# Decay-row loads of a state-space stage, issued from GpSimd's queue instead of SyncE's

## The chip, the cores and the metric

The kernel is one program on one core of a Trainium2 chip. Five engines run their own instruction streams in order and meet at semaphores: TensorE (PE, with its weight loads shown as PEld), VectorE (DVE), ScalarE (ACT), GpSimd (POOL) and SyncE (SP). The metric is the device time of one execution in microseconds (us); before the change the median of three runs was 1223.0 us (1222.05 to 1225.13). All data is float32, and products are made with the input split into a high and a low part (`split`), so that one float32 product is three matmuls.

## The reference

One decoder layer with two token mixers on 1024 tokens of width 1024. The part that the change touches is the state-space branch: 16 heads of 64, state size 64, chunks of 128 tokens.

```python
a_cs = jnp.cumsum(ac, axis=-1)                       # per head and chunk
seg = a_cs[..., :, None] - a_cs[..., None, :]
lmat = jnp.exp(jnp.where(tril, seg, -jnp.inf))       # decay between two tokens of a chunk
cb = jnp.einsum("bclgn,bcsgn->bgcls", cc, bc)
y_diag = jnp.einsum("bgrcls,bcsgrp->bclgrp", cb[:, :, None] * lmat, xc)
decay_states = jnp.exp(a_cs[..., -1:] - a_cs)
states = jnp.einsum("bclgn,bgrcl,bclgrp->bcgrpn", bc, decay_states, xc)
...                                                  # states carried from chunk to chunk
y_off = jnp.einsum("bclgn,bcgrpn,bgrcl->bclgrp", cc, prev_states, jnp.exp(a_cs))
y = y_diag + y_off + d_skip * xs
```

Around it stand the input norm and the input projection to 8472 columns ahead of it, and behind it attention with forget gates, the projections of both branches, gates, the output projection and a last norm.

## The kernel before

The program runs in stages: norm and first projections (to about 100 us), the other projections as Strassen-like pair products (to about 480 us), the state-space stage with the last projections mixed in (about 480 to 722 us), attention (to about 930 us) and the output products. A scheduler places all instructions of the build into one order per engine by a timeline of its own, with priorities; an engine then runs its list strictly in order. The state-space stage has priority 300 over the rest (`tc.high_priority(offset=SPRI)`), and projection slabs of v, q and k (`fill`, called from `FILL`) give TensorE work between its steps.

The stage's work is 4 groups of heads (`qd`), each of 2 halves (`hf`), each of 4 chunks (`c`): 32 chunks in all, done by `ssd_half`. One chunk goes like this.

- `ab` (128x512, 3 buffers) is filled from DRAM (`a_scr`) with the four decay rows of the chunk, copied to all 128 partitions (L688). ScalarE makes four relus (L690) and one exp (L692) of it, VectorE multiplies it with `cb` (L693), and `split` turns it into `m4`: a cast on ScalarE (L98) and a subtraction on VectorE (L99, `m<-ab,m`). That subtraction is the last reader of the `ab` buffer, and so releases it for the chunk three later.
- TensorE transposes the chunk of x (`xs`) into `xps` (L698). VectorE makes `xd` (L707) and `xe` (L710) of it, and both are split.
- L718 makes the chunk's addition to the state, L724 updates the state `st32` on VectorE, and `sn` is its split (cast on ScalarE, subtraction on VectorE). The next chunk's L746 and L747 need `sn`.
- L735 makes the part inside the chunk (12 small matmuls), L746 and L747 the part from the state carried over. VectorE multiplies the latter with `eb` (L748) and adds the former (L751). `eb` (2 buffers) holds decay rows too, loaded by two DMAs for each chunk but the first of a group (L740), 56 in all.

After a half, VectorE adds the skip (L779), multiplies by the gate (L780) and sums the squares (L785, `sacc`). After the last half TensorE adds these up in two groups of columns (L791, shown as 8 instructions each), VectorE scales (L794), GpSimd takes a power (L796), TensorE transposes (L798), and the result goes out and comes back as `rb` for the attention stage.

All DMAs of the program are issued from SP. In the stage these are the loads of `ab`, `eb`, `xs`, `zt` (the gate) and `wr` (weights of the projection slabs), and the stores of results. SP waits, at each issue, until the buffer is free and the DMA that used the same completion semaphore before has landed; what stands behind waits too. GpSimd has nothing to do between 30 us and L796 at 722.7 us.

Of the kernel before, what the change touches and what calls it, by code (L numbers as in the profile page):

```python
# [31 lines left out]
P = 128  # L32
# [33 lines left out]
def build(ctx, tc, t):  # L66
    nc = tc.nc
    V, A, G, PE, SP = nc.vector, nc.scalar, nc.gpsimd, nc.tensor, nc.sync
# [88 lines left out]
    a_scr = dram.tile([P, P], F32, name="a_scr")  # L157
# [479 lines left out]
    with tc.tile_pool(name="sd", bufs=1, side="right") as sd, \  # L637
            tc.tile_pool(name="sdp", bufs=1, space=PSUM) as sdp:

        def sp():  # L640
            return sdp.tile([P, 512], F32, tag="sp", bufs=4, name="sp")
# [36 lines left out]
        def ssd_half(qd, hf, xs, ys, st32, sn):  # L678
# [3 lines left out]
            for c in range(4 * hf, 4 * hf + 4):  # L682
                tk = slice(c * P, (c + 1) * P)
                th = slice((c % 4) * P, (c % 4 + 1) * P)
                r0 = c * 16 + 4 * qd
                m4 = sd.tile([P, 2, 4, P], F32R, tag="m4", bufs=3, name="m4")
                ab = sd.tile([P, 4, P], F32, tag="ab", bufs=3, name="ab")
                SP.dma_start(out=ab, in_=a_scr[r0:r0 + 4].rearrange("(o h) l -> o h l", o=1).broadcast_to([P, 4, P]))  # L688
                for i in range(4):
                    A.activation(out=ab[:, i, :], in_=ab[:, i, :], func=AF.Relu, scale=-1.0,  # L690
                                 bias=acs[:, c, 4 * qd + i:4 * qd + i + 1])
# [39 lines left out]
                for i in range(4):  # L731
                    o = yd[0:64, (i % 2) * 256 + (i // 2) * P:(i % 2) * 256 + (i // 2) * P + P]
# [4 lines left out]
                if c > 0:  # L737
                    eb = sd.tile([P, 2, P], F32, tag="eb", bufs=2, name="eb")
                    for z in range(2):
                        SP.dma_start(out=eb[z * 64:(z + 1) * 64],  # L740
                                     in_=e_scr[r0:r0 + 4].rearrange("(r two) l -> two r l", two=2)[z:z + 1]
                                     .broadcast_to([64, 2, P]))
                    yo = sp()
                    for i in range(2):
                        ps_ = slice(i * P, (i + 1) * P)
                        PE.matmul(yo[:, ps_], lhsT=so[:, ps_], rhs=ch[g][:, tk], start=True, stop=False)  # L746
                        PE.matmul(yo[:, ps_], lhsT=so[:, ps_], rhs=cl[g][:, tk], start=False, stop=True)  # L747
                    V.tensor_tensor(out=ys[:, :, th], in0=yo[:, 0:256].rearrange("p (r l) -> p r l", r=2), in1=eb,  # L748
                                    op=ALU.mult)
                    for z in range(2):  # L750
                        V.tensor_tensor(out=ys[half[z], :, th], in0=yd[z], in1=ys[half[z], :, th], op=ALU.add)  # L751
                else:
                    for z in range(2):
                        A.copy(out=ys[half[z], :, th], in_=yd[z])
# [9 lines left out]
        for qd in range(4):  # L764
            st32, sn = sd.tile([P, 256], F32, tag="st32", bufs=1, name="st32"), None
            for hf in range(2):
                hs = slice(hf * 512, (hf + 1) * 512)
                xs = [sd.tile([P, 512], F32, tag="xs", bufs=5, name="xs") for _ in range(2)]
                for i in range(2):
                    SP.dma_start(out=xs[i], in_=x_scr[2 * qd + i][:, hs])  # L770
                ys = sd.tile([P, 2, 512], F32, tag="ys", bufs=2, name="ys")
                with tc.high_priority(offset=SPRI):
                    sn = ssd_half(qd, hf, xs, ys, st32, sn)
                for i in range(2):
                    j = 2 * qd + i
                    zt = sd.tile([P, 512], F32, tag="zt", bufs=2, name="zt")
                    SP.dma_start(out=zt, in_=z_scr[j][:, hs])
                    y = ys[:, i]
                    V.scalar_tensor_tensor(out=y, in0=xs[i], scalar=dskip[:, j:j + 1], in1=y, op0=ALU.mult, op1=ALU.add)  # L779
                    V.tensor_tensor(out=y, in0=y, in1=zt, op=ALU.mult)  # L780
                    if j == 0:
                        A.activation(out=sacc[:, hs], in_=y, func=AF.Square)
                    else:
                        A.activation(out=zt, in_=y, func=AF.Square)
                        V.tensor_tensor(out=sacc[:, hs], in0=sacc[:, hs], in1=zt, op=ALU.add)  # L785
                    SP.dma_start(out=u_scr[j][:, hs], in_=y)
            for f in FILL[qd]:
                fill[f]()
# [461 lines left out]
```

## Time and profile before

| | |
|---|---|
| median of 3 runs (lowest, highest) | 1223.0 us (1222.05, 1225.13) |
| the profiled execution's own time | 1224.68 us |
| its span (first to last instruction) | 1223.0 us |
| mean granted TensorE clock | 0.987 |
| busy in the span: PE / DVE / ACT / POOL | 95% / 78% / 52% / 7% |
| busy in 600 to 700 us, inside the stage: PE / DVE / ACT / POOL | 94.8% / 93.3% / 67.0% / 0% |

A row of a timeline has the start in us, the duration in us, the engine, the line, the operation, what it writes and reads, how many instructions were merged, and in brackets how long the engine was idle before it and what ended that wait. Matmuls overlap, so that the distance from one start to the next tells TensorE's pace, and the duration does not. Waits are put down to what came last.

### The profile page before, as it was taken

Reading aid. Unit: us, or ns where it says so; the run is one execution under the profiler, and the core shown is the slowest. Engines: PE = TensorE matmul, PEld = TensorE weight load, DVE = VectorE, ACT = ScalarE, POOL = GpSimd, SP = SyncE. Lnnn points to the kernel's source line nnn. Section 1 sums busy time; section 2 is a strip of 40 time slices with the busy share of each in tenths; the row PEclk is TensorE's granted clock in tenths of the full one; section 3 lists DMA queues with packets and bytes.
Section 4 is the critical chain, followed back from the end, with each engine's and each line's share of the span. In section 5 each row is a group of like instructions: output and inputs, shape, how many; then the busy total and the mean of one; then the engine's idle time right before and its main releaser. Section 6 shows DMA issues by size and latency. Waiting matters only on the chain.

```text
span 1223.0 us, 18391 instructions
## 1 busy us (share of the span) xinstructions
PE 1162.5 (95%) x6206; PEld 978.0 (80%) x6206; DVE 952.6 (78%) x1942; ACT 634.6 (52%) x1260; POOL 87.8 (7%) x152
## 2 busy tenths in 40 slices
PE   3999999999999999999998989999989998999997
PEld 2788888788877878998887878888868886788876
DVE  5857699788887774599999976664677967979967
ACT  7554443444453334876676633443556644454465
POOL 1000000000000000000000012222322220000001
PEclk9999999999999999999999989999999999999999
DMA  9764643655485665656555658431255627955334
GB/s 371 262 247 162 220 141 102 208 198 181 151 288 175 229 235 198 195 155 212 186 167 158 220 202 297 138 112 53 91 183 184 190 70 250 326 181 181 104 96 147
DMA packets 109018, 228.26 MB, mean 187 GB/s; under 512 B 12362, under 2 KB 20220, under 8 KB 107900
## 3 DMA queue, kind: packets, MB, share of 16 engines
q1 hardware_dynamic: 108924, 227.09, 55.5%
q8 instruction: 49, 0.80, 0.3%
q14 instruction: 45, 0.37, 0.1%
HBM read 159.14 MB, written 67.90 MB: 186 GB/s over the span
## 4 chain that ended last, share of the span: by engine, by line
PE 71%; DVE 12%; DMA 9%; issue 4%; ACT 3%; SPq 0%; POOL 0%; POOLq 0%; DVEq 0%; ACTq 0%
PE pp L497 5%; PE pp L499 5%; PE pp L500 5%; PE pv L1061 4%; PE mm L497 4%; PE mm L499 4%; PE mm L500 4%; PE mm L112 3%; PE mm L113 3%; PE mm L111 3%; PE lg L1030 3%; PE tp L1051 2%; PE mm L915 2%; PE mm L913 2%; DMA ab<-a_scr 2%
## 5 line engine op out<-in xcount | busy, mean ns | idle before, releaser
L98 ACT CAST wh<-wr 128x512 fp32r<-128x512 f32 (+1 forms) x214 | 131.0, 619 | 172.4 <-DMA wr<-w_c 33.2
L99 DVE TENSOR_TENSOR wl<-wr,wh 128x512 fp32r<-128x512 f32 (+1 forms) x214 | 145.6, 686 | 43.3 <-ACT wh L98 42.8
L112 PE MATMUL mm<-hl,wh 128*128 128x512 f32 x288 | 116.6, 405 | 0.4 <-DVE hl L306 0.4
L111 PE MATMUL mm<-hh,wh 128*128 128x512 f32 x288 | 116.0, 408 | 0.0
L113 PE MATMUL mm<-hh,wl 128*128 128x512 f32 x288 | 115.3, 401 | 0.0
L136 PE MATMUL mm<-wh,hh 128*128 128x256 f32 (+1 forms) x256 | 73.0, 287 | 2.2 <-DVE tmp L348 2.2
L137 PE MATMUL mm<-wl,hh 128*128 128x256 f32 (+1 forms) x256 | 73.7, 289 | 0.0
L138 PE MATMUL mm<-wh,hl 128*128 128x256 f32 (+1 forms) x256 | 73.0, 286 | 0.0
L1036 ACT ACTIVATE pr<-pr,sm 128x1024 f32<-128x1024 f32 (+3 forms) x64 | 49.9, 780 | 43.8 <-DVE sm L1035 36.6
L1054 ACT CAST pth<-tp 128x512 fp32r<-128x512 f32 (+1 forms) x80 | 42.4, 543 | 51.0 <-PE tp L1051 42.7
L1031 DVE CUSTOM_DVE_ANT_0 pr<-lg,fb 128x512 f32<-128x512 f32 (+1 forms) x96 | 51.3, 550 | 18.2 <-PE lg L1030 12.4
L112 PEld LDWEIGHTS mm<-hl,wh 128*128 128x128 f32 x288 | 55.1, 191 | 11.0 <-DVE hl L306 1.0
L113 PEld LDWEIGHTS mm<-hh,wl 128*128 128x128 f32 x288 | 55.0, 191 | 10.4
L111 PEld LDWEIGHTS mm<-hh,wh 128*128 128x128 f32 x288 | 54.7, 192 | 10.2 <-ACT hh L305 0.3
L690 ACT ACTIVATE ab<-ab,acs 128x128 f32<-128x128 f32 x128 | 41.2, 391 | 40.6 <-DMA ab<-a_scr 35.7
L1055 DVE TENSOR_TENSOR ptl<-tp,pth 128x512 fp32r<-128x512 f32 (+1 forms) x80 | 49.9, 630 | 11.1 <-ACT pth L1054 10.7
L1039 POOL TENSOR_SCALAR pr<-pr,sm 128x1024 f32<-128x1024 f32 (+3 forms) x64 | 51.9, 812 | 86.9 <-DVE sm L1038 67.1
L98 ACT CAST sh<-sr 128x512 fp32r<-128x512 f32 x57 | 33.9, 618 | 42.1 <-DVE sr L479 30.6
L796 POOL TENSOR_TENSOR fl<-fl,mhalf 128x8 f32<-128x8 f32 x1 | 1.6, 1647 | 696.5 <-DVE fl L794 696.5
L136 PEld LDWEIGHTS mm<-wh,hh 128*128 128x128 f32 x256 | 48.1, 188 | 2.6 <-DVE tmp L348 2.4
L1061 PE MATMUL pv<-pth,vh 128*128 128x256 f32 (+1 forms) x160 | 45.8, 286 | 4.2 <-DVE zg L1064 3.6
L138 PEld LDWEIGHTS mm<-wh,hl 128*128 128x128 f32 x256 | 48.3, 189 | 0.0
(406 smaller groups left out, 3496.2 us busy)
## 6 DMA issues: line engine op xcount, KB each, us to landing
wr<-w_c SPq DMA_DIRECT2D x116, 256.0 KB, 3.8
wa<-w_ada SPq DMA_DIRECT2D x8, 1024.0 KB, 11.4
g_scr<-gt SPq DMA_DIRECT2D x16, 512.0 KB, 4.0
ab<-a_scr SPq DMA_DIRECT2D x32, 256.0 KB, 4.2
gt<-g_scr SPq DMA_DIRECT2D x32, 256.0 KB, 3.7
wr<-w_ps SPq DMA_DIRECT2D x28, 256.0 KB, 2.8
wr<-w_pa SPq DMA_DIRECT2D x28, 256.0 KB, 2.7
wr<-so SPq DMA_DIRECT2D x28, 256.0 KB, 2.7
```

Of the source, the lines that this page charges most:

```text
L98: A.copy(out=hi[:, :n], in_=raw[:, :n])
L99: eng.tensor_tensor(out=lo[:, :n], in0=raw[:, :n], in1=f32(hi[:, :n]), op=ALU.subtract)
L111: PE.matmul(ps, lhsT=hi[:, cs], rhs=xh[k][:, hs], start=(k == 0), stop=False)
L112: PE.matmul(ps, lhsT=hi[:, cs], rhs=xl[k][:, hs], start=False, stop=False)
L113: PE.matmul(ps, lhsT=lo[:, cs], rhs=xh[k][:, hs], start=False, stop=(k == 7))
L136: PE.matmul(o, lhsT=xh[k][:, ts], rhs=hi[:, cs], start=(k == 0), stop=False)
L137: PE.matmul(o, lhsT=xh[k][:, ts], rhs=lo[:, cs], start=False, stop=False)
L138: PE.matmul(o, lhsT=xl[k][:, ts], rhs=hi[:, cs], start=False, stop=(k == 7))
L497: PE.matmul(ps, lhsT=f[0][:, w], rhs=xh[:, hs], start=(first and k == 0), stop=False, skip_group_check=True)
L499: PE.matmul(ps, lhsT=f[0][:, w], rhs=xl[:, hs], start=False, stop=False, skip_group_check=True)
L500: PE.matmul(ps, lhsT=f[1][:, w], rhs=xh[:, hs], start=False, stop=(k == 3), skip_group_check=True)
L1061: PE.matmul(pv[:, o0:256], lhsT=x[kb // 4][:, kb % 4, vs], rhs=y[:, d:d + m], start=(kb == 0 and i == 0), stop=(kb == 2 * qq + 1 and i == 2))
```

## The change

The two places that load decay rows, 32 DMAs of `ab` (256 KB each) and 56 of `eb` (64 KB each), are issued from GpSimd's queue.

```diff
-                SP.dma_start(out=ab, in_=a_scr[r0:r0 + 4].rearrange("(o h) l -> o h l", o=1).broadcast_to([P, 4, P]))
+                G.dma_start(out=ab, in_=a_scr[r0:r0 + 4].rearrange("(o h) l -> o h l", o=1).broadcast_to([P, 4, P]))
...
                     for z in range(2):
-                        SP.dma_start(out=eb[z * 64:(z + 1) * 64],
+                        G.dma_start(out=eb[z * 64:(z + 1) * 64],
                                      in_=e_scr[r0:r0 + 4].rearrange("(r two) l -> two r l", two=2)[z:z + 1]
                                      .broadcast_to([64, 2, P]))
```

The scheduler places every instruction anew, so the order changes on all engines within this stage and for a short while after it. At three places the rows read as follows.

SP, at the start of the stage (lines with a minus stand in the order before, with a plus in the order now; `xs` are the first two chunks' inputs of x, `wr` a weight, `g_scr` a store of the stage ahead):

```order
 L185 DMA g_scr_110<-gt 128x1024
 L85 DMA wr<-w_c 128x512
-L688 DMA ab<-a_scr 128x512 x2
-L740 DMA eb<-e_scr 64x2x128 x2
-L688 DMA ab<-a_scr 128x512
-L740 DMA eb<-e_scr 64x2x128 x2
-L185 DMA g_scr_109<-gt 128x1024
 L770 DMA xs<-x_scr_204 128x512
 L770 DMA xs<-x_scr_205 128x512
+L185 DMA g_scr_109<-gt 128x1024
```

The loads of `xs` now follow directly on the weight, with seven loads of decay rows and one store no longer ahead of them.

TensorE, around the first transpose of x (L698) in the order before (L136 to L138 are the projection of v; `hh_240` to `hh_247` and `hl_248` to `hl_255` are the eight slices of the input that each of its products goes through, three matmuls a slice):

```order
L138 MATMUL mm<-wh,hl_253 128x256
L136 MATMUL mm<-wh,hh_246 128x256
L137 MATMUL mm<-wl,hh_246 128x256
L138 MATMUL mm<-wh,hl_254 128x256
L136 MATMUL mm<-wh,hh_247 128x256
L137 MATMUL mm<-wl,hh_247 128x256
L698 MATMUL xp<-ident,xs 128x128
L138 MATMUL mm<-wh,hl_255 128x256
```

And the same place in the order now:

```order
L136 MATMUL mm<-wh,hh_242 128x256
L137 MATMUL mm<-wl,hh_242 128x256
L138 MATMUL mm<-wh,hl_250 128x256
L136 MATMUL mm<-wh,hh_243 128x256
L137 MATMUL mm<-wl,hh_243 128x256
L138 MATMUL mm<-wh,hl_251 128x256
L698 MATMUL xp<-ident,xs 128x128
L667 MATMUL sp<-ch_4525,m_4529 128x128
```

Counted from the start of the projection of v in this stage, 95 of its matmuls stand ahead of the first L698 in the order before and 60 now: it moved forward past 35 of them. The transposes of the next four chunks moved by 35 to 40.

TensorE, at the end of the stage in the order before (L746 and L747 are the last chunk's, L791 the sums of squares, L111 to L113 the last projection slab, whose products go through the same eight slices, twice, with one half after the other):

```order
L113 MATMUL mm<-hh_244,wl 128x512
L746 MATMUL sp<-ch_4526,sn 128x128
L747 MATMUL sp<-cl_4528,sn 128x128
L746 MATMUL sp<-ch_4526,sn 128x128
L747 MATMUL sp<-cl_4528,sn 128x128
L791 MATMUL sp<-ones,sacc 128x1 x4
L111 MATMUL mm<-hh_245,wh 128x512
L112 MATMUL mm<-hl_253,wh 128x512
```

And now:

```order
L112 MATMUL mm<-hl_249,wh 128x512
L746 MATMUL sp<-ch_4526,sn 128x128
L747 MATMUL sp<-cl_4528,sn 128x128
L746 MATMUL sp<-ch_4526,sn 128x128
L747 MATMUL sp<-cl_4528,sn 128x128
L113 MATMUL mm<-hh_241,wl 128x512
L111 MATMUL mm<-hh_242,wh 128x512
L112 MATMUL mm<-hl_250,wh 128x512
L791 MATMUL sp<-ones,sacc 128x1 x4
```

In both orders the slab then runs to its end, and the second group of L791 and L798 follow on it. Before, three slices of the first half and the whole second half were left behind the last L746 (9 + 24 = 33 matmuls); now one matmul, six slices and the second half are (1 + 18 + 24 = 43).

## Rows read from the trace of the kernel before

**Rows 1.** Busy time by stretch, with instruction counts; PEclk, DMA share and GB/s last.
```profile
520.00:600.00 80.00, 79.85 (x616) 72.65 (x616) 74.31 (x187) 58.99 (x154) 0.00 (x0) 1.00 0.58 180
600.00:700.00 100.00, 94.82 (x680) 82.71 (x680) 93.30 (x224) 67.00 (x164) 0.00 (x0) 1.00 0.59 183
```

**Rows 2.** Waits of PE in 480 to 722 us: total, times, longest.
```profile
PE sp L746 <- DVE sn L99: 2.1, 3, 0.9
PE xp L698 <- DMA xs<-x_scr: 1.7, 2, 1.0
...
```

**Rows 3.** Timeline of SP at the start of the stage, and in its middle.
```profile
488.87 1.07 SPq L688 DMA_DIRECT2D ab<-a_scr  x2
...
491.96 1.56 SPq L740 DMA_DIRECT2D eb<-e_scr  x2
...
494.20 3.37 SPq L770 DMA_DIRECT2D xs<-x_scr  x2
...
642.64 0.33 SPq L688 DMA_DIRECT2D ab<-a_scr  x1
```

**Rows 4.** Timeline of PE at four places of the stage.
```profile
501.28 0.33 PE L698 MATMUL xp<-ident,xs 128*128 128x128 f32 x1 [0.66 <-DMA xs<-x_scr]
...
602.99 0.28 PE L137 MATMUL mm<-wl,hh 128*128 128x256 f32 x1
...
605.71 0.28 PE L136 MATMUL mm<-wh,hh 128*128 128x256 f32 x1
...
712.41 0.30 PE L746 MATMUL sp<-ch,sn 128*128 128x128 f32 x1
...
714.06 0.39 PE L112 MATMUL mm<-hl,wh 128*128 128x512 f32 x1
...
721.24 0.39 PE L113 MATMUL mm<-hh,wl 128*128 128x512 f32 x1
721.47 0.95 PE L791 MATMUL sp<-ones,sacc 128*128 128x1 f32 x8
724.40 0.27 PE L798 MATMUL sp<-ident,fl 128*8 128x128 f32 x1 [1.99 <-POOL fl L796]
```

**Rows 5.** Timeline of DVE: start, middle and end of the stage, and attention.
```profile
502.47 0.42 DVE L707 TENSOR_TENSOR xd<-xp,dt 128x256 f32<-128x256 f32 x1 [6.42 <-PE xp L698]
...
641.93 0.68 DVE L99 TENSOR_TENSOR m<-ab,m 128x512 fp32r<-128x512 f32 x1
...
711.84 0.42 DVE L99 TENSOR_TENSOR sn<-st,sn 64x256 fp32r<-64x256 f32 x1 [0.54 <-ACT sn L98]
...
718.72 1.48 DVE L785 TENSOR_TENSOR sacc<-sacc,zt 128x512 f32<-128x512 f32 x2
...
837.89 1.22 DVE L99 TENSOR_TENSOR kl<-qt,kh 128x1024 fp32r<-128x1024 f32 x1
```

**Rows 6.** The tile ab: issues, who waited for its load, landing.
```profile
L688 SPq DMA_DIRECT2D ab<-a_scr x32: 319/326/732, 488.9 to 679.3; - x32
...
  DMA ab<-a_scr: 35.7, 22
...
DMA to landing us min/median/max: 3.0/4.2/7.7
```

**Rows 7.** The tile eb: its issues, in ns.
```profile
L740 SPq DMA_DIRECT2D eb<-e_scr x56: 573/597/1033, 490.0 to 709.5; - x56
```

**Rows 8.** Chain that ended last, 560 to 780 us: first and last load of ab.
```profile
575.32 6.39 DMA ab<-a_scr
...
679.27 4.15 DMA ab<-a_scr
```

**Rows 9.** GpSimd's dearest small instruction: busy us, mean ns, idle before.
```profile
L796 POOL TENSOR_TENSOR fl<-fl,mhalf 128x8 f32<-128x8 f32 x1 | 1.6, 1647 | 696.5 <-DVE fl L794 696.5
```

**Rows 10.** Timeline of POOL in attention, one form twice.
```profile
830.18 0.29 POOL L1022 TENSOR_SCALAR_AFFINE_SELECT fb<-fb 128x128 f32<-128x128 f32 x1 [0.67 <-DVE sm L1038]
...
838.05 1.22 POOL L1022 TENSOR_SCALAR_AFFINE_SELECT fb<-fb 128x128 f32<-128x128 f32 x1 [6.24 <-DVE sm L1031]
```

## The prediction

> **What bounds the kernel now.** I read the busy time by stretch first. Through the state-space stage TensorE is busy nearly all the time (79.85 of 80 us, then 94.82 of 100), and VectorE almost as much (74.31 of 80, then 93.30 of 100); ScalarE has a third free in 600 to 700 us (67.00), and GpSimd does nothing [rows 1]. So two engines are near their limit together, and a faster load can be worth no more than the time in which these two wait. Next the waits of TensorE: in 480 to 722 us it has six entries that add up to 5.9 us, the two largest being 2.1 us for `sn` and 1.7 us for the load of `xs` [rows 2]. Those 5.9 us, 0.5% of the time, are the whole that the change can win within the stage. Then the load itself: `ab` lands a median of 4.2 us after its issue (3.0 to 7.7), and ScalarE waited for it 22 times, 35.7 us in all [rows 6]. The chain that ended last passes through a load of `ab` five times between 575 and 680 us; the first took 6.39 us and the last 4.15 [rows 8], and the five together 23.1 us. So these loads hold up ScalarE, through it VectorE, and TensorE only where the projection slabs give no more cover. Last the ends of the stage. At its start VectorE sat idle 6.42 us until the first transpose of x, which itself waited 0.66 us for `xs` [rows 4, 5]. At its end the last `sn` was ready at 712.26 and TensorE used it at 712.41, with 0.15 us to spare; then it ran projections without a gap to 721.47, while VectorE had finished the sums at 720.2, 1.27 us ahead of the L791 that reads them [rows 4, 5].
>
> **The start.** SP issued the three `ab` and four `eb` loads from 488.87 to 493.52 and one store behind them, and `xs` only from 494.20 [rows 3]. With those seven gone from SP, `xs` can be issued some 5 us earlier, and the first L698 stands 35 matmuls earlier in TensorE's order. The pace of these is 23 steps from 602.99 to 605.71, 0.118 us each [rows 4], so 35 x 0.118 = 4.1 us. VectorE's 6.42 us of idle time shrinks by that, and as the engine with the least room it keeps the 4.1 us unless something else holds it. The wait of 0.66 us for the first `xs` goes as well.
>
> **The end.** The last chunk's L746 stands 10 projection matmuls earlier (43 behind it instead of 33). Their pace is 31 steps from 714.06 to 721.24, 0.232 us each [rows 4]: 10 x 0.232 = 2.3 us. If VectorE delivered `sn` at 712.26 as before, TensorE would meet it at about 710.1, wait 2.3 us, and still have all 43 to do: the stage would end 2.3 us later. With VectorE 4.1 us ahead it has 4.1 - 2.3 = 1.8 us to spare, and I take those 1.8 us off TensorE's waits for VectorE. What follows L791 (L794, the power on GpSimd, L798, with TensorE idle 1.99 us before it [rows 4]) has the same order and the same cost; GpSimd's last loads stand ahead of L796, but were all due before the sums.
>
> **The loads.** SP is spared 32 x 0.326 + 56 x 0.597 = 43.9 us of issuing [rows 6, 7]. Inside the stage that is worth nothing: an `ab` was issued as soon as its buffer came free (VectorE's last read of one ended at 641.93 + 0.68 = 642.61, and SP issued at 642.64 [rows 3, 5]), so that the queue waited for VectorE, and GpSimd's will. What an issue costs on GpSimd no row shows, since no DMA is issued there. Bounds from the nearest rows: from below, a load that has no other transfers ahead of it lands as the fastest did, 3.0 us, a gain of 1.2; from above, as the slowest, 7.7 us, a loss of 3.5 [rows 6]. Between them I add to the median GpSimd's dearest small instruction in place of SP's issue: 1.65 - 0.33 = +1.3 us [rows 6, 9]. Against this the order gives more room: between the cast of one chunk's `ab` and the first relu of the chunk three later (29 such pairs) ScalarE has 9.2 instructions on average before and 11.6 now. At 67.00 us / 164 = 0.41 us an instruction [rows 1] the 2.4 more cover 1.0 us. So +1.3 - 1.0 = +0.3 us a load, and over the five passages of the chain +1.5 us. Three issues a chunk of 1.65 us are 5 us in a chunk of 6.9 (from 501.28 to 721.47 us, 32 of them [rows 4]), on an engine that is otherwise empty. Should that cover be gone, because an `ab` stands behind two `eb` loads on GpSimd, it is 3.3 us late.
>
> The Trainium skill ("DMA: Bandwidth & Descriptors", section "Latency and other measured facts") gives about 1 us to the first byte from GpSimd against 0.6 us from SP. By it alone the term would be +0.4 instead of +1.3 a load, within what the order covers, and the loads would cost nothing. No run here shows it yet.
>
> **The sum.** -0.7 (first `xs`) - 1.8 (the rest of TensorE's waits) + 1.5 (the loads) = -1.0 us. The profiled execution took 1224.7 us, its span 1223.0, so it would be 1223.7; it ran 1.7 us above the median. Against the median of 1223.0 I predict 1222.0 us. That is within 0.3% (3.7 us), about what a measurement of this kernel can tell from no change.
>
> **Rivals.** *Loads that pass the others.* The five loads on the chain took 23.1 us, one of them 6.39 with stores and gate loads issued just ahead on SP's queue [rows 8]. If a queue of their own let each land in 3.0 us, 8.1 us would leave the chain, and TensorE could lose all its 5.9 us of waits: 1217 us. For it speaks that spread of 3.0 to 7.7 us; against it, that TensorE must meet no other wait, and VectorE has only 12 us of idle time left in 520 to 700 us [rows 1].
>
> *GpSimd held up by VectorE (slower).* In attention one and the same GpSimd instruction took 0.29 us at 830.18 and 1.22 us at 838.05, while VectorE ran L99 with two inputs from SBUF from 837.89 to 839.11 [rows 5, 10]: GpSimd seems to have stood until that ended. In the state-space stage VectorE runs such instructions most of the time. If an issue on GpSimd is held up in the same way, each costs 0.9 us more, and `ab` is at 4.2 + 1.3 + 0.9 = 6.4 us, 1.2 us beyond what the order covers: 5 x 1.2 = 6 us on the chain. With `eb` loads held up ahead of it, it reaches the upper bound of 7.7 us: 5 x (3.5 - 1.0) = 12.5 us. With the gains at the start spent, that is 1229 to 1235 us. It decides from a landing of about 5.2 us, the old median and the 1.0 us that the order gives; from there ScalarE stands for each load, and `sn` is late for L746.
>
> The Trainium skill ("SBUF — State Buffer", section "SBUF: two separate sides") states a rule against this change: DMAs issued from GpSimd need descriptors that it writes itself, and VectorE in a mode with two ports locks it out, so that loads seem blocked by VectorE. For instructions with two SBUF inputs it says the lock holds only against GpSimd work that reads SBUF. By the first half the result is this rival's 1229 to 1235, by the second the 1222 above; the stretched row agrees with the lock, but the instruction in it does read SBUF, so that no row decides for descriptors.
>
> *An end without its start (same).* VectorE doesn't keep the 4.1 us, since ScalarE's relus or the first `ab` arrive later, and the 10 matmuls at the end stand: 1223 - 0.7 + 2.3 = about 1225 us.
>
> **How the numbers follow.** I give the forecast, with the third rival as its slow edge, 47% (own range 1219.3 to 1226.7), passing loads 25% (1216 to 1219), held-up issues 28% (1227 to 1235). Faster by over 0.3% is 0.25, within 0.47, slower 0.28. The range reaches from 1217 (all of TensorE's waits gone) to 1233 (most of the way to the upper bound for the loads), which leaves out some 5% below and 10% above.
>
> **What would show it.** Right: VectorE's wait before its first `xd` falls from 6.4 us to 2 or 3; the first L698 runs near 497 us; the last L746 starts 2 to 4 us earlier in the stage, and L798 stays within 3 us of 724.4; `ab` lands in 4.5 to 5.7 us, and ScalarE's wait for it stays near 35.7 us. The passing loads would show as a landing near 3 us and waits of TensorE under 2 us. Held-up issues would show as issues on GpSimd of over 2 us that end with VectorE's instructions, ScalarE's wait for `ab` at 60 us or more, and TensorE waiting for `sn` by more than 8 us. The forecast is wrong if attention and what follows change, since nothing there was touched but a few places in the order.

## The result, and the profile after

Over 20 runs of each, the median went from 1223.87 to 1227.25 us, a ratio of 1.0027 (95% interval 1.0016 to 1.0038): 3.3 us slower. In a later comparison (11 runs against 29) it was 1.0013 (0.9998 to 1.0029). The prediction was 1222.0 us, 1.0 us faster. The profiled execution took 1225.39 us, with a span of 1223.7 us.

I look first at the stage that the change touches. These are TensorE's waits in 480 to 722 us of the changed kernel (total, times, longest); they answer to [rows 2]:

```profile
PE sp L746 <- DVE sn L99: 2.7, 2, 2.5
PE xp L698 <- DVE xd L707: 0.7, 1, 0.7
PE xp L698 <- DMA xs<-x_scr: 0.6, 2, 0.3
```

They add up to 4.0 us, against 5.9 before. The longest of them is a new one, inside the stage and not at its end:

```profile
660.51 0.48 PE L746 MATMUL sp<-ch,sn 128*128 128x128 f32 x1 [2.46 <-DVE sn L99]
```

VectorE's timeline at the start of the stage, where it sat idle 6.42 us before [rows 5]:

```profile
496.81 0.42 DVE L707 TENSOR_TENSOR xd<-xp,dt 128x256 f32<-128x256 f32 x1 [1.16 <-PE xp L698]
```

TensorE's timeline at the end of the stage; L798 stood at 724.40 [rows 4]:

```profile
722.45 0.37 PE L798 MATMUL sp<-ident,fl 128*8 128x128 f32 x1 [2.02 <-POOL fl L796]
```

The last `sn`, ready at 706.53, and the L746 of the last chunk that uses it (712.26 and 712.41 before [rows 4, 5]):

```profile
706.11 0.42 DVE L99 TENSOR_TENSOR sn<-st,sn 64x256 fp32r<-64x256 f32 x1 [0.55 <-ACT sn L98]
```

```profile
708.18 0.22 PE L746 MATMUL sp<-ch,sn 128*128 128x128 f32 x1
```

And the tile `ab` (durations in ns, least, median, most; then who waited for its load, and its landing), answering to [rows 6]:

```profile
L688 POOL DMA_DIRECT2D ab<-a_scr x32: 546/592/774, 489.0 to 674.9; - x32
...
  ACT ab L690: 31.7, 19
...
DMA to landing us min/median/max: 3.3/4.3/11.0
```

So in this execution the stage ended 2.0 us earlier than in the profile before, and an issue on GpSimd cost 0.59 us. The lead held to the last instruction of VectorE, L1159, here in the changed kernel and then before:

```profile
1215.62 0.75 DVE L1159 SCALAR_TENSOR_TENSOR b<-b,qq,fw 128x512 f32<-128x512 f32 x1 [0.66 <-POOL qq L1158]
```

```profile
1218.29 0.75 DVE L1159 SCALAR_TENSOR_TENSOR b<-b,qq,fw 128x512 f32<-128x512 f32 x1 [0.66 <-POOL qq L1158]
```

Yet the span is 0.7 us longer. What is left is the end of the program. Each engine closes with a DRAIN, put down to the last line, L1246. Rows of that line, durations in ns (least, median, most), first and last start; the changed kernel:

```profile
L1246 POOLq DRAIN  x3: 40/102/7870, 1215.0 to 1223.4; - x3
L1246 SPq DRAIN  x3: 7/7/7, 1219.5 to 1223.1; - x3
```

The kernel before:

```profile
L1246 POOLq DRAIN  x3: 34/78/657, 1217.7 to 1222.7; - x3
L1246 SPq DRAIN  x3: 7/7/7, 1222.2 to 1222.5; - x3
```

The row to look at is the longest DRAIN of GpSimd (POOLq): 7.87 us from 1215.0, thus until 1222.9, where before it took 0.66 us. (Its record starts while GpSimd's last power, L1158, still runs for 0.55 us, which is most of the 0.66.) SP came to its own DRAIN at 1219.5, once the output stores had landed, and then had to wait. Before, SP's was the last, at 1222.2. From the end of VectorE's last instruction (its start and 0.75 us) to the end of the span it is 7.35 us now and was 3.95 us: 3.4 us lost behind the last piece of real work.

### The profile page after: what moved, and what is told of

It reads as the page before. It is cut to its first block, busy times and chain, and to the rows that moved or that the text cites. A ratio compares the mean times of both kernels' runs of the same rounds, so it can differ in the third digit from the quotient of the medians.

```text
span 1223.7 us, 18423 instructions
## 1 busy us (share of the span) xinstructions
PE 1162.8 (95%) x6206; PEld 980.2 (80%) x6206; DVE 952.8 (78%) x1942; ACT 634.9 (52%) x1260; POOL 140.1 (11%) x240
## 4 chain that ended last, share of the span: by engine, by line
PE 65%; DVE 13%; DMA 9%; issue 7%; ACT 4%; POOL 1%; SPq 1%; POOLq 0%; DVEq 0%; ACTq 0%
PE pv L1061 4%; PE mm L112 4%; PE mm L113 4%; PE mm L111 4%; PE pp L497 4%; PE pp L499 4%; PE pp L500 4%; PE lg L1030 4%; PE mm L497 3%; PE mm L499 3%; PE mm L500 3%; PE tp L1051 3%; DMA wr<-w_c 2%; PE mm L915 2%; PE mm L913 2%
## 5 line engine op out<-in xcount | busy, mean ns | idle before, releaser
L111 PE MATMUL mm<-hh,wh 128*128 128x512 f32 x288 | 116.7, 410 | 0.0
L113 PE MATMUL mm<-hh,wl 128*128 128x512 f32 x288 | 116.1, 404 | 0.0
L688 POOL DMA_DIRECT2D ab<-a_scr x32 | 18.7, 586 | 560.5 <-DMA bc<-x_scr 462.3
L136 PE MATMUL mm<-wh,hh 128*128 128x256 f32 (+1 forms) x256 | 72.9, 286 | 1.8 <-DVE tmp L348 1.8
L138 PE MATMUL mm<-wh,hl 128*128 128x256 f32 (+1 forms) x256 | 73.4, 288 | 0.0
L113 PEld LDWEIGHTS mm<-hh,wl 128*128 128x128 f32 x288 | 55.6, 193 | 10.6
L111 PEld LDWEIGHTS mm<-hh,wh 128*128 128x128 f32 x288 | 55.2, 194 | 10.1 <-ACT hh L305 0.3
L690 ACT ACTIVATE ab<-ab,acs 128x128 f32<-128x128 f32 x128 | 41.2, 391 | 32.6 <-DMA ab<-a_scr 31.7
L136 PEld LDWEIGHTS mm<-wh,hh 128*128 128x128 f32 x256 | 48.1, 189 | 2.2 <-DVE tmp L348 2.0
L137 PEld LDWEIGHTS mm<-wl,hh 128*128 128x128 f32 x256 | 48.2, 189 | 0.2
L138 PEld LDWEIGHTS mm<-wh,hl 128*128 128x128 f32 x256 | 48.3, 189 | 0.0
```

The costliest lines, as they stand in the source:

```text
L111: PE.matmul(ps, lhsT=hi[:, cs], rhs=xh[k][:, hs], start=(k == 0), stop=False)
L113: PE.matmul(ps, lhsT=lo[:, cs], rhs=xh[k][:, hs], start=False, stop=(k == 7))
L136: PE.matmul(o, lhsT=xh[k][:, ts], rhs=hi[:, cs], start=(k == 0), stop=False)
L137: PE.matmul(o, lhsT=xh[k][:, ts], rhs=lo[:, cs], start=False, stop=False)
L138: PE.matmul(o, lhsT=xl[k][:, ts], rhs=hi[:, cs], start=False, stop=(k == 7))
```

## The experiments

Theory: the DRAIN costs 3.4 us in every run, because GpSimd's queue has carried DMAs; the stage itself is worth little. Rivals: its length goes with the number of DMAs and not with any use; the loss lies in the stage; the DRAIN waits for something else.

**One load, 32 loads, 56 loads.** `e1_one_load` moves the gate bias alone, `e4_ab_only` and `e8_eb_only` one of the two lines of the change (L688 alone, L740 alone).

```diff
-            SP.dma_start(out=gbias[:, :D], in_=t["b_gate_ada"].broadcast_to([P, D]))
+            G.dma_start(out=gbias[:, :D], in_=t["b_gate_ada"].broadcast_to([P, D]))
```

> The kernel before with one load moved to GpSimd's queue: the gate bias (L568, once, at about 368 us); the order on TensorE, VectorE and ScalarE is that of before. Theory (the end): once GpSimd's queue has carried a DMA, the DRAIN that ends GpSimd's program takes about 7.9 us from its last instruction (0.66 us in the kernel before), whatever the number of DMAs. Then one load is enough: DRAIN 7 to 8 us, about 7.3 us from the last instruction of VectorE to the end of the span instead of 4.0, ratio near 1.0027 (+3.3 us). Rival A (the DRAIN grows with the number of DMAs, 88 in the changed kernel): DRAIN under 1 us, ratio 1.000. Rival B (the loss is inside the state-space stage, the long DRAIN only looks like it): whatever the DRAIN takes, ratio 1.000.

> Of the change only the 32 loads of ab on GpSimd's queue, the 56 of eb on SP as before. Theory (the end, whatever the number of DMAs): DRAIN 7 to 8 us, 7.3 us from VectorE's last instruction to the end; xs no longer stands behind three ab loads but still behind four eb loads, so that less than the 4.1 us at the start is won; ratio 1.001 to 1.003. Rival A (the DRAIN grows with the number): 0.66 + 7.2 x 32 / 88 = 3.3 us, hidden beside the output stores, ratio 0.998 to 1.000.

> Of the change only the 56 loads of eb on GpSimd's queue, the 32 of ab on SP as before. Theory: last DRAIN 0.66 + 56 x 0.082 = 5.25 us; the output stores are in 4.5 us after GpSimd's last instruction (1219.5 less 1215.0 in the changed kernel), so that 0.7 us of the DRAIN shows at the end; xs behind three loads of ab instead of seven loads; ratio 0.9995 to 1.0010. Rival (bytes decide: eb is 64 KB a load, ab 256 KB, so 56 eb are 30% of the bytes): DRAIN 0.66 + 0.3 x 7.2 = 2.8 us, ratio below 1.000.

Measured: a DRAIN of 0.752, 3.289 and 5.258 us. My first theory (any use costs 7.9 us) fell; the rival that the DRAIN grows with the number had said 3.3 and 5.25. The ratios were 0.9987 (0.9970 to 1.0003), 0.9991 (0.9976 to 1.0005) and 1.0009 (0.9988 to 1.0031), and the end of the span came 4.05, 3.95 and 4.65 us behind VectorE: up to 32 loads the DRAIN hides beside the output stores, with 56 it shows by 0.7 us.

**GpSimd finished early.** `e2_after_power_on_act` takes the last power off GpSimd, `e3_before_power_on_act` does the same to the kernel before.

```diff
-            G.tensor_tensor(out=qq[:, tb, 1:2], in0=qq[:, tb, 1:2], in1=mhalf[:, 0:1], op=ALU.pow)
+            A.activation(out=qq[:, tb, 1:2], in_=qq[:, tb, 1:2], func=AF.Abs_reciprocal_sqrt)
```

> The changed kernel with its last power (L1158, eight 128x1) moved from GpSimd to ScalarE as an inverse root, so that GpSimd's last instruction stands in attention at about 1011 us and its DRAIN can run beside the rest. Theory (the end): the DRAIN still takes 7 to 8 us but from about 1011 us, the span ends some 4 us after VectorE's last instruction as in the kernel before, and the time falls by some 3.4 us against the changed kernel; with the 2.7 us that the profile shows won before the end the ratio to before is 0.998 (if these 2.7 us belong to the one profiled execution, up to 1.000). Rival B (the loss is in the body): 1.003 as the changed kernel. Rival C (the DRAIN waits for the stores or for the other engines and not for GpSimd's own queue): it ends at 1222 to 1223 again and the ratio stays at 1.003.

> Control for the run with the power on ScalarE: the kernel before with the same move of L1158 and nothing else. Each of the last powers takes 0.55 us on GpSimd and some 0.2 to 0.3 on ScalarE, so all theories expect 0 to -0.5 us (ratio 0.9995 to 1.000), a DRAIN of GpSimd far from the end, and 4.0 us from VectorE's last instruction to the end.

Measured: the DRAIN stood at 1020.1 us and took 7.70 us there (0.48 in the control), though GpSimd had been without a DMA for some 300 us: idle time alone did not shorten it. It was off the path, and the span ended 5.15 us behind VectorE, in the control 5.05. The ratios were 1.0005 (0.9984 to 1.0025) and, for the control, 1.0014 (0.9996 to 1.0032) where I had expected no loss; with the move the span ends about 1 us later behind VectorE than before, and whether that costs time the interval does not tell. That the DRAIN was over at 1027.8 us rules out that it waits for the last stores or the other engines; the times alone don't prove 3.4 us.

**The DRAIN paid earlier.** `e5_drain_early` was to do that and failed: the scheduler put the added DRAIN at 1.1 us, ahead of all loads (last DRAIN 7.872 us, ratio 1.0013, 0.9996 to 1.0031). It is one more profile of the changed stage. `e9_drain_pinned` holds it behind the last load. The edits of the two:

```diff
-        G.tensor_tensor(out=rc, in0=rc, in1=mhalf, op=ALU.pow)
+        G.tensor_tensor(out=rc, in0=rc, in1=mhalf, op=ALU.pow); G.drain()
```

```diff
-        rps = sp()
+        rps = sp(); tc.keep_in_program_order(G.drain())
```

> The changed kernel with one more DRAIN on GpSimd, right behind the power L796 that follows the state-space stage; TensorE and GpSimd keep the order of the changed kernel. Theory as it stands after the first runs (the last DRAIN takes 0.66 us and 0.082 us for each DMA that GpSimd has issued and not yet accounted for: 0.66, 0.75, 3.29 and 7.87 us for 0, 1, 32 and 88 loads): the early DRAIN takes about 7.9 us from about 724 us, where GpSimd has next to nothing to do, the last one falls to about 0.7 us, the span ends about 4 us after VectorE's last instruction, and the time is that of the changed kernel less 3.4 us: ratio to before 1.000 (0.998 if the 2.7 us that the profile showed before the end are there in most executions). Rival (the last DRAIN goes over all DMAs of the program whether or not an earlier one did): last DRAIN 7.9 us again, ratio 1.003.

> The run with an early DRAIN again, as that one stood at the start of the program (1.1 us) and so tested nothing: now the DRAIN is held behind GpSimd's last load of the stage and ahead of the power L796. Every engine has the order of the changed kernel. Theory: the DRAIN takes some 7.9 us from about 713 us, within the 14 to 15 us that GpSimd waits there for L794; the last DRAIN is near 0.7 us; the span ends 4.0 us after VectorE's last instruction instead of 7.3, and the time is 3.3 us below that of the changed kernel run beside it (ratio to before about 1.000). Rival (the last DRAIN goes over all DMAs whether or not an earlier one did): last DRAIN 7.9 us, ratio as the changed kernel, 1.003.

> The changed kernel once more, as the measure for the early DRAIN beside it and for the spread of its stage. Its first profile showed the stage 2 us shorter than before; two later kernels with the same order in the stage showed it 3 us longer, with TensorE waiting 4.8 to 5.5 us for xs (0.6 in the first profile), because xs and the first loads of ab land in 10 to 12 us where the loads of both queues start together. If that is the rule: wait for xs 3 to 6 us, first ab issue to L798 237 to 240 us (before 235 to 236), last DRAIN 7.87 us, ratio 1.003. If the first profile is the rule: wait for xs under 1 us and 233 us.

The DRAINs of `e9_drain_pinned`, the added one (L789) and those of the end:

```profile
L789 POOLq DRAIN  x1: 8785/8785/8785, 704.2 to 704.2; - x1
```

```profile
L1246 POOLq DRAIN  x3: 34/102/652, 1213.4 to 1218.5; - x3
L1246 SPq DRAIN  x3: 7/7/7, 1217.9 to 1218.2; - x3
```

The cost moved to 704.2 us, where GpSimd waits for L794 anyway; the last DRAIN is 0.65 us, and the span ends 3.95 us behind VectorE, as before the change. Beside it, `e12_after_again` (the changed kernel unaltered) had 7.872 and 7.25 us. The ratios were 1.0002 (0.9984 to 1.0019) and 1.0013 (0.9998 to 1.0029). So the end's 3.3 us are shown in the traces; of the times, the difference of the medians is 1.8 us and the intervals overlap, since the stage varies by more. The held DRAIN took 8.79 us and not the 7.9 that were expected; part of that is the last `eb` issue, which ran until 705.0, and the rest is open.

**Why the stage varies.** Five profiles have the changed order in the stage. From the first issue of `ab` to L798 they took 233.4 and 233.1 us (the first one and `e9_drain_pinned`), but 238.7, 239.4 and 240.9 us in `e2_after_power_on_act`, `e5_drain_early` and `e12_after_again`. Three profiles with the order before took 234.6 to 236.3. Busy time by stretch at the start of the stage in `e12_after_again` (PE, PEld, DVE, ACT, POOL, then granted clock, DMA share, GB/s):

```profile
490.00:495.00 5.00, 5.00 (x44) 5.00 (x43) 3.66 (x3) 4.90 (x6) 4.31 (x7) 1.00 1.02 361
495.00:500.00 5.00, 2.42 (x21) 2.22 (x19) 1.22 (x1) 4.90 (x9) 0.00 (x0) 1.00 0.98 247
500.00:505.00 5.00, 4.71 (x28) 4.72 (x29) 0.85 (x2) 3.35 (x10) 0.00 (x0) 0.66 0.78 250
```

And its waits of TensorE in 488 to 722 us:

```profile
PE xp L698 <- DMA xs<-x_scr: 3.5, 2, 2.9
PE sp L746 <- DVE sn L99: 3.1, 1, 3.1
PE xp L698 <- DVE xd L707: 2.5, 1, 2.5
```

The same stretches in the first profile of the changed kernel:

```profile
490.00:495.00 5.00, 5.00 (x44) 5.00 (x44) 4.23 (x4) 4.88 (x6) 3.33 (x6) 1.00 0.95 303
495.00:500.00 5.00, 4.92 (x43) 4.72 (x42) 1.70 (x4) 4.90 (x10) 0.00 (x0) 1.00 1.00 229
500.00:505.00 5.00, 5.00 (x45) 5.00 (x45) 4.65 (x15) 5.00 (x17) 0.00 (x0) 1.00 0.92 312
```

With both queues issuing at once the 16 DMA engines are full (0.95 to 1.02 from 490 to 500 us; with one queue, before, 0.95 and 0.86), and the first five loads of `xs` take 4.9 to 12.0 us to land in the first profile and 5.6 to 13.0 in the later one, against 4.9 to 7.0 before. What parts short from long is the second of them: it landed in 7.3 and 7.4 us in the two short cases and in 10.4 to 10.9 in the three long ones. L698 stands 35 matmuls earlier and meets it or doesn't. Where it doesn't, TensorE stops for 2.9 to 3.4 us. In `e12_after_again` the granted clock in the 5 us in which that stop ends is 0.66, between the full 2.4 GHz and its lower level of 1.2 GHz, so that TensorE also runs slower for a while; in `e2_after_power_on_act` it stayed at 1.00 after a stop of 3.1 us. In the long cases TensorE waited 3.5 to 5.5 us for `xs` in all, in the short ones 0.6 and 0.8.

All five profiles share the other stop, the one at 660.51 in the first: 2.5 to 3.1 us at an L746 between 660 and 671 us, where the order before had at most 0.93 (665.72). The stretches around it in the first profile:

```profile
655.00:660.00 5.00, 3.05 (x26) 2.45 (x24) 3.06 (x8) 3.25 (x9) 0.65 (x2) 1.00 0.38 128
660.00:665.00 5.00, 4.49 (x14) 3.91 (x15) 4.86 (x13) 3.58 (x10) 2.36 (x5) 0.53 0.32 104
665.00:670.00 5.00, 5.00 (x30) 4.10 (x30) 4.86 (x10) 3.46 (x8) 1.17 (x2) 0.79 0.50 183
```

After the stop the clock fell, here to 0.53, near its lower level, in the three long cases to 0.50 to 0.68; in `e9_drain_pinned` it stayed at 1.00. In the three profiles with the order before it was 1.00 there. What this stop costs the stage I did not isolate.

I tried to remedy the wait for `xs` with its loads in four parts of 32 partitions (`e15_xs_parts`):

```diff
-                    SP.dma_start(out=xs[i], in_=x_scr[2 * qd + i][:, hs])
+                    [SP.dma_start(out=xs[i][z:z + 32], in_=x_scr[2 * qd + i][z:z + 32, hs]) for z in range(0, P, 32)]
```

> The changed kernel with each load of xs in four parts of 32 partitions, on SP as before. The scheduler puts the stage in another order than in the changed kernel. If the wait for xs at the start decides whether the stage is long, and parts land sooner as those of ab did (3.2 us instead of 4.3): TensorE's wait for xs under 2 us, first ab issue to L798 near 233 us, last DRAIN 7.87 us, ratio 0.999 to 1.001. If the DMA engines are simply full there (0.95 to 1.02 busy from 490 to 505 us): xs lands as late as before, wait 3 to 5 us, stage 239 us, ratio 1.001 to 1.003.

It missed: the wait was 5.2 us, the stage 236.3, the ratio 1.0054 (1.0035 to 1.0074), worse than either case. That full DMA engines delay `xs` is not shown: no run took the load off them with all else kept, and they were as full in the short cases, and in `e7_more_loads` below (0.95 and 1.05), where the second `xs` landed in 5.6 us and TensorE did not wait for one. Why that load is late in three profiles of five stays open.

**Only the first loads.** `e6_first_loads` keeps the ten loads of the first half of the first group on GpSimd:

```diff
-                SP.dma_start(out=ab,
+                (G if qd + hf == 0 else SP).dma_start(out=ab,
...
-                        SP.dma_start(out=eb[z * 64:(z + 1) * 64],
+                        (G if qd + hf == 0 else SP).dma_start(out=eb[z * 64:(z + 1) * 64],
```

> Only the ten decay loads of the first half chunk row (four of ab, six of eb) on GpSimd's queue, the other 78 on SP as before. It keeps what the change does at the start of the stage (xs no longer behind seven loads) without the long DRAIN. Theory: last DRAIN 0.66 + 10 x 0.082 = 1.5 us, hidden beside the output stores; the first L698 some 4 to 6 us earlier, against an end of the stage that may be some 2 us worse, so -1 to -2.7 us: ratio 0.998 to 0.999. Rival (the gain at the start was of the one profiled execution, or is given back at the end of the stage): 1.000. Rival (each load on GpSimd lands later and costs more than the start wins): over 1.000.

The DRAIN was 1.502 us, as said. VectorE's first `xd` ran at 498.24 after 0.87 us of idle time, so the start was won; but the ratio was 1.0045 (1.0024 to 1.0066), with ScalarE waiting 49.3 us for `ab` (35.7 before), TensorE 4.0 us for `xs` (1.7 before) and the stage 238.5 us long. A gain at the start is given back inside the stage. By the prediction's own measure the order left the loads less room: between the cast of one chunk's `ab` and the first relu of the chunk three later ScalarE has 8.4 instructions, before 9.2. Which edge of the new order costs the time I did not isolate.

**More and smaller loads.** `e7_more_loads` splits each `ab` into four loads on GpSimd (184 in all), `e13_two_parts` into two (120), `e14_four_parts_ab_only` into four with `eb` back on SP (128), `e11_parts_on_sp` into four with everything on SP; `e10_parts_and_drain` is the first of these with the held DRAIN.

```diff
-                G.dma_start(out=ab, in_=a_scr[r0:r0 + 4].rearrange("(o h) l -> o h l", o=1).broadcast_to([P, 4, P]))
+                [G.dma_start(out=ab[z:z + 32], in_=a_scr[r0:r0 + 4].rearrange("(o h) l -> o h l", o=1).broadcast_to([32, 4, P])) for z in (0, 32, 64, 96)]
```

> The changed kernel with each load of ab in four parts of 32 partitions, all on GpSimd's queue: 4 x 32 + 56 = 184 DMAs for the same bytes. Theory (0.082 us a DMA in the last DRAIN): 0.66 + 184 x 0.082 = 15.7 us, which puts the end 7.9 us later than in the changed kernel; GpSimd has 96 more issues of some 0.59 us in the stage (57 us of 225), which it has free, so the ratio is 1.009 (1.008 to 1.012). Rival (the DRAIN grows with the bytes or the packets and not with the DMAs): DRAIN near 7.9 us, ratio 1.003.

> The changed kernel with each load of ab in two parts of 64 partitions on GpSimd's queue: 64 + 56 = 120 loads. Theory 1 (0.082 us a load whatever its size, up to some number above 120): last DRAIN 0.66 + 120 x 0.082 = 10.5 us, 6 us beyond the output stores. Theory 2 (small loads cost the DRAIN less: 128 parts cost 0.6 us in the run with 184, 0.005 each): 0.66 + 56 x 0.082 + little = 5.3 to 5.9 us. Theory 3 (loads are accounted for when the number reaches a bound, and the DRAIN has the rest): below 5 us or near 10.5, but not by size. Of the stage: parts of 128 KB land between 3.2 and 4.3 us, ScalarE waits 10 to 25 us for ab, ratio 0.996 to 1.001 with theory 2, 1.001 to 1.004 with theory 1.

> Only ab on GpSimd's queue, in four parts (128 loads), eb on SP as before. Theory 1 (a bound between 120 and 128, or a DRAIN of the rest): whatever is left of 128, under 7 us or, without a bound, 0.66 + 128 x 0.082 = 11.2 us. Theory 2 (small loads cost little): 0.66 + 0.6 = 1.2 us. Of the stage: if the gain of the run with 184 loads comes from ab landing in parts, ScalarE's wait for it stays under 8 us and the ratio is 0.993 to 0.996; if eb has to leave SP as well, 0.996 to 1.000.

> The kernel before (all decay loads on SP) with each load of ab in four parts of 32 partitions. It tells whether the parts or GpSimd's queue won in the run with 184 loads. If the parts (a part lands sooner than the whole, on any queue): ab lands near 3.2 us instead of 4.2, ScalarE's wait for it falls from 35.7 us to under 10, ratio 0.994 to 0.997. If both are needed (SP has 96 issues of 0.33 us more, 31 us, and xs stands behind nine more of them at the start of the stage, 3 us): ratio 0.998 to 1.002.

> The kernel with ab in four parts on GpSimd's queue (184 DMAs, 0.995), with the same DRAIN held behind the last load of the stage. Theory: its last DRAIN of 5.83 us showed by some 1.3 us beyond the output stores; that goes: ratio 0.994 (0.992 to 0.996). If the early DRAIN stands in the way of L796 it shows as a longer wait of TensorE before L798 than 2.0 us and the ratio is not below 0.995.

| kernel | loads on GpSimd | last DRAIN, us | VectorE's end to span's end, us | ratio to before |
|---|---|---|---|---|
| `e13_two_parts` | 120 | 10.485 | 9.85 | 1.0031 (1.0015 to 1.0046) |
| `e14_four_parts_ab_only` | 128 | 11.124 | 10.55 | 1.0038 (1.0022 to 1.0055) |
| `e7_more_loads` | 184 | 5.830 | 5.25 | 0.9949 (0.9932 to 0.9965) |
| `e10_parts_and_drain` | 184 | 0.652 | 4.05 | 0.9947 (0.9933 to 0.9961) |
| `e11_parts_on_sp` | 0 | 0.657 | 3.85 | 0.9991 (0.9978 to 1.0004) |

Up to 128 loads the DRAIN is 0.66 us and 0.08 to 0.1 us for each load, of 64, 128, 256 or (one load) 512 KB alike ((11.124 - 0.657) / 128 = 0.082, and 10.5 was forecast for 120). My forecast of 15.7 us for 184 was wrong: the 5.83 are worth 63 loads, as if some 121 no longer counted at the end. The DRAIN held at 703.1 us in `e10_parts_and_drain` took 7.76 us for the same 184. What happens between 128 and 184 stays open. With 120 and 128 loads the span ends 5.9 and 6.6 us later behind VectorE than in the kernel before, and the time is 3.8 and 4.7 us longer: most of a long DRAIN goes into the time, though these kernels have stages of their own order.

The other surprise is the 6.2 us won by `e7_more_loads`. Its tile `ab`:

```profile
L688 POOL DMA_DIRECT2D ab<-a_scr x128: 498/498/724, 488.3 to 684.6; - x128
...
  ACT ab L690: 1.5, 2
...
DMA to landing us min/median/max: 2.1/3.2/8.4
```

Two rows of its timeline, one load's issues and the first read of the same load:

```profile
605.60 2.00 POOL L688 DMA_DIRECT2D ab<-a_scr  x4 [3.13 <-DVE m L99]
```

```profile
616.03 1.29 ACT L690 ACTIVATE ab<-ab,acs 128x128 f32<-128x128 f32 x4
```

And the pair at about the same place in the changed kernel:

```profile
606.23 0.56 POOL L688 DMA_DIRECT2D ab<-a_scr  x1 [5.08 <-DVE m L99]
```

```profile
609.61 1.28 ACT L690 ACTIVATE ab<-ab,acs 128x128 f32<-128x128 f32 x4 [0.54 <-DMA ab<-a_scr]
```

Here 10.4 us lie between issue and read instead of 3.4; the median over the 32 loads is 10.5 us, in the changed kernel 4.6, before 4.2, with two parts 5.5, and with four parts on SP 4.8. With 10 us of lead hardly a load is late (1.5 us of ScalarE's waits in the stage instead of 31.7), TensorE waits 1.0 us in all, and the stage takes 227.7 us, with the DRAIN held 229.2. The room stands in ScalarE's order: between the cast of one chunk's `ab` and the first relu of the chunk three later stand 21.8 instructions on average in `e7_more_loads` and in `e10_parts_and_drain`, against 11.6 in the changed kernel, 12.3 with two parts, 16.0 with four parts and `eb` on SP, and 11.6 with four parts on SP. In the last three ScalarE still waited 33.7, 20.7 and 27.7 us for `ab`; for two parts 10 to 25 had been forecast, for four parts with `eb` on SP under 8. So neither the queue alone (88 loads there lose) nor the size of a part alone (on SP they land in 2.6 us, sooner than the whole, and win nothing beyond the interval) explains the gain. The order that the two together drew from the scheduler fits these counts; but no run kept that order and changed the loads, so this is argued and not shown. `e10_parts_and_drain` is as fast as `e7_more_loads` and free of the long DRAIN at the end; the 1.2 us by which this shortens the end don't show in the times. Both are faster than the kernel before, clear of their intervals.

## Why the prediction was wrong, step by step

- **Start.** The mechanism was right: `xs` issued at 488.5, the first L698 at 495.4 (497 was said), VectorE's idle time 1.16 us (2 to 3 said). But "it keeps the 4.1 us unless something else holds it", said of VectorE, left out what did hold it in three of five profiles: the second load of `xs`, with VectorE idle 3.9 to 4.2 us. "The wait of 0.66 us for the first `xs` goes as well": there the first wait for an `xs` grew to 2.9 to 3.4 us.
- **End of the stage.** The step held. In the first profile the last `sn` was ready at 706.53 and its L746 ran at 708.18, 1.65 us later, where 1.8 us to spare had been worked out; in none of the five profiles did the last chunk's L746 wait for `sn`. All waits of TensorE together fell by 1.9 us in the first profile, of the 2.5 (0.7 for `xs` and 1.8) that I took off. What the prediction did not have is a wait that the new order adds: it put new waits of TensorE inside the stage at nothing, and the L746 at 660 to 671 us cost 2.5 to 3.1 us in each of the five, with the granted clock falling behind it in four. The order had been compared at three places, and this is not one of them.
- **Loads.** Mis-sized to the safe side: an issue costs 0.59 us and not 1.65, landing went from 4.2 to 4.3 us and not to 5.5, ScalarE's wait from 35.7 to 31.7 us (33.3 to 36.8 in the other four profiles). The Trainium skill ("DMA: Bandwidth & Descriptors", section "Latency and other measured facts") was nearer with its 0.4 us more for a DMA from GpSimd.
- **GpSimd held up by VectorE** did not happen: no issue of the 88 took over 0.78 us, with VectorE busy 95.6 of 100 us in 600 to 700. Of the two statements that the prediction takes from the Trainium skill ("SBUF — State Buffer", section "SBUF: two separate sides") the trace agrees with the second one, that VectorE's instructions with two SBUF inputs lock out only GpSimd work that reads SBUF.
- **The step that failed** is the sum, which ended at L798: "What follows L791 ... has the same order and the same cost". From L798 to VectorE's last instruction that held (493.2 us, before 493.9). Behind it GpSimd's program ends with a DRAIN whose cost the 88 loads raise from 0.66 to 7.87 us, 3.4 us of them past the output stores. With it the sum would have been -1.0 + 3.4 = +2.4 us; 3.3 were measured (2.0 to 4.7). The sign that the prediction gave for itself, "wrong if attention and what follows change", is the one that came, behind the last instruction. The -1.0 us for the stage is not confirmed either: the stage was 2 us shorter in two profiles and 3 to 5 us longer in three than the 235.5 us before, and without the long DRAIN at the end `e9_drain_pinned` ran at 1.0002 (0.9984 to 1.0019) of the time before. That the first profile showed the stage 2.0 us shorter was luck, two cases of five. No row ahead of the prediction shows a GpSimd that had issued a DMA, but the row of GpSimd's last DRAIN could have been read and asked what it waits for. The 28% for slower went to a mechanism that did not show; the rival for the end of the program was missing.

## What to carry to other kernels

Moving DMAs to GpSimd's queue lengthened the DRAIN that closes its program: look at what an engine does between its last instruction and the end of the span, and either keep its DMAs few enough for the output stores to cover (some 45 here by estimate: 0.66 + 45 x 0.082 = 4.3 us, where the stores were in 4.5 us after the DRAIN began) or pay the DRAIN in a gap of that engine. A load that is hidden needs lead, not a faster queue: compare the time from issue to first read with the landing. An order compared at three places says nothing of the others: ask where else an engine may now stand and wait. And one profile of a stage that depends on a race of loads is one throw: take several before you credit it with 2 us.

## What the runs showed of the hardware

- The DRAIN at the end of GpSimd's program: 0.66, 0.75, 1.50, 3.29, 5.26, 7.87, 10.49 and 11.12 us with 0, 1, 10, 32, 56, 88, 120 and 128 DMAs issued by GpSimd; 5.83 us with 184. After one in the middle of the program (8.79 us at 704.2) the last took 0.65 us; some 300 us without DMAs did not shorten it (7.70 us).
- An issue on GpSimd took 0.59 us for 256 KB and 0.50 us for 64 KB of the same rows, on SP 0.33 us for 256 KB [rows 6].
- In the stage, in the five profiles of the changed order, TensorE stopped nine times for 2.5 to 3.4 us. After seven of these stops the granted clock fell, to a mean of 0.50 to 0.77 in the lowest stretch of 5 us (a stop of 2.9 us: 0.66); after two, of 2.7 and 3.1 us, it stayed at 1.00.
